# A trunk layer on one core: more weight blocks in the first stage, context tiles in a later pool, constant products first

## The chip, the core and the metric

The kernel runs on one core of a Trainium2 chip. It is one launch. The time is that of the whole execution on the device, in microseconds (us); the kernel before was run three times. PE is the matrix engine, DVE the vector engine, ACT the scalar engine, POOL the engine called GpSimd, SP the engine that issues most transfers. Each of them runs its own instructions strictly in the order in which they were put, and waits at an instruction until what it needs is there.

## The reference

One layer of a backbone over 512 latent tokens and 256 context tokens of width 1024. Cut to what matters:

```python
mx = adaln(c, w_mod, b_mod, 6)            # silu(c) @ w_mod: six rows of 1024
mc = adaln(c_ctx, w_mod, b_mod, 2)
hx = modulate(rmsnorm(x, norm1_g), mx[0], mx[1])
hc = modulate(rmsnorm(ctx, norm1_g), mc[0], mc[1])
s5p = s5_discretize(...)                  # parameters of the state-space branch
xa, xb, xcg, ux, qx, kx, vx, ga, gb, gc = split_in(hx @ w_in)
uc = hc @ w_in[:, S5 columns]
kc, vc = split(hc @ w_in[:, key and value columns])
ya = short_conv_branch(xa, xb, xcg, conv_w, conv_out)
yb = s5_output(ux, states of the scan over uc and ux, ...)
yc = neighbourhood_attention(qx, kx, vx, kc, vc, rpb) @ na_out
x = x + mx[2] * ((sigmoid(ga) * ya + sigmoid(gb) * yb + sigmoid(gc) * yc) @ w_out)
x = x + mx[5] * (relu(modulate(rmsnorm(x, norm2_g), mx[3], mx[4]) @ w1) ** 2 @ w2)
return rmsnorm(x, final_norm_g)
```

Everything is float32. A product of two float32 matrices is made of three matmuls of rounded parts: high by high, high by low, low by high.

## The kernel before, in words

**Weights.** All weights stand in the chip's memory as one stream of blocks of 1 MB, in the order of use; a block has two halves. SP fetches a block as soon as its buffer is free (`fetch`, L130 to L147). The first ten blocks belong to the first stage; they rotate through three buffers, two called raw and one rawx, so that block b waits until both halves of block b-3 are used. From block 10 on there are the two raw buffers alone. `wsplit` (L156) makes the high part wh of a half on ACT (L171) and the low part wl on DVE (L174); a unit of work then is 24 matmuls.

**First stage.** Eight steps d, one for each 128 channels. A step computes two columns of the modulation (`st_mod`, L511: 16 matmuls with 2 rows out, tile mod, which has one PSUM buffer), copies the row on ACT (L515, mrow), turns it on PE (L520) and adds constants on DVE (`st_col`, L521 to L523: colS, colA, modc). With the columns, DVE makes xr (L543), ACT its high part (L544, rg), DVE its low part (L549), and PE multiplies by the weights of the state-space input (st_m and st_a). The first xr needs the norm of x: four squares on ACT (L400), folds on DVE (L401, L405), a sum on PE (xcs), the root rcx on ACT (L411), a diagonal xdg on DVE (L372) and PE's xps (L373). The next step's `st_mod` is issued before this step's products.

**Beside it** DVE works through the parameters of the state-space branch (`gen_par`, L247 to L343, about a hundred small instructions; the sines are on ACT, L279). Its factors CFcr, CFnci, CFar and CFai feed `gen_s5e`: for each of eight blocks POOL makes products e, ta and tb (L421) and their sums (L457, L466), PE the lag products kps (L435) and the transposes etps (L442). With the last kps, DVE adds the kf rows (L479). `gen_ctx` is the norm of the context: the tile cxr (L558), squares on ACT, sums on POOL (L584 to L586, csq), PE's cps, then eight products and eight low parts on DVE (L378, L380). `gen_s5c` makes eight C blocks from transfers cb (L490), blocks 0 to 4 on DVE, 5 to 7 on POOL (tiles c and tc), and writes each to C_d.

**After it** come units in the order xa, cg, xb, uc, ga and cv and so on, with the state-space stage (stps, yps), the attention and the MLP. uc are the four context units.

The order of each engine's instructions is not written by hand: the program issues the work in the order of the code, generators being pumped between the units, and a scheduler with a model of the times then sets each engine's order. Tiles live in pools; a pool opened in the space of a closed one waits until the old tiles are no longer read. The rawx buffers, cxr and the tiles of the norms are in the start pool stp; it is closed when `gen_ctx` is through. RG are eight tiles of high and low parts of normalised channels; RG0 to RG3 hold those of the latent tokens.

Of the kernel before, what the change touches and what calls it, by code (L numbers as in the profile page):

```python
# [9 lines left out]
F32 = mybir.dt.float32  # L10
F32R = mybir.dt.float32r
I32 = mybir.dt.int32
AF = mybir.ActivationFunctionType
# [5 lines left out]
D = 1024  # L19
T = 512  # L20
TC = 256
# [54 lines left out]
def trunk(tc, xT, ctxT, cond, condT, vecs, wst, s5p, s5bc, dmat, biasA, outT):  # L76
    nc = tc.nc
# [25 lines left out]
    es = ExitStack()  # L103
    with es:
# [14 lines left out]
        def pss(name):  # L119
            return pp.tile([128, 512], F32, tag="s", bufs=1, name=name)  # L120
# [3 lines left out]
        NST = 10  # L124
        nblk = len(STREAM) // 2
# [4 lines left out]
        def fetch():  # L130
            b = st_next[0]
            back = 3 if b < NST else RAWB
            if b < nblk and (b < back or used[b - back] == 2):
                if b < NST and b % 3 == 2:
                    raws[b] = stp.tile([128, 2048], F32, tag="rawx", bufs=1, name=f"raw{b}")
                else:
                    raws[b] = wp.tile([128, 2048], F32, tag="raw", bufs=RAWB, name=f"raw{b}")
                if b < 2:
                    for o in (0, 1024):
                        nc.sync.dma_start(raws[b][:, o:o + 1024], wst[b][:, o:o + 1024])  # L140
                else:
                    nc.sync.dma_start(raws[b], wst[b])
                st_next[0] += 1
                return True
            return False
# [36 lines left out]
        RG = [gp.tile([128, 2048], F32R, name=f"rg{i}") for i in range(8)]  # L182
# [19 lines left out]
        nc.scalar.dma_start(silx, cond[0:1, :].to_broadcast([128, D]))  # L202
# [148 lines left out]
        S.activation(dum, epsc, AF.Silu)  # L351
        for _ in range(5):
            next(gpar)
# [38 lines left out]
        S.activation(silx, silx, AF.Silu)  # L392
        S.activation(dum, silx[:, 0:1], AF.Square)
# [164 lines left out]
        cxr = stp.tile([128, 8, TC], F32, tag="rawx", bufs=1, name="cxr")  # L558
        nc.sync.dma_start(cxr, ctxT)
# [19 lines left out]
        def gen_ctx():  # L579
            sq, sq2 = (stp.tile([128, 4, TC], F32, tag="sq", bufs=3, name=f"csq{i}") for i in range(2))  # L580
# [6 lines left out]
            cS = stp.tile([128, 8], F32, name="cS")  # L587
            cA = stp.tile([128, 8], F32, name="cA")
# [4 lines left out]
            rsc = rms("c", sq[:, 0], TC, stp, pss("cps"))  # L593
# [524 lines left out]
        gc = gen_ctx()  # L1118
# [11 lines left out]
        stp_cm.__exit__(None, None, None)  # L1130
# [305 lines left out]
```

## Time and profile before

| | |
|---|---|
| median of 3 runs | 1051.85 us (1051.36 to 1053.2) |
| profiled execution | 1054.51 us |
| its span, first to last instruction | 1052.7 us |
| mean granted PE clock | 0.979 |
| PE busy | 1004.4 us, 95% of the span |
| DVE, ACT, POOL busy | 558.9, 366.7, 200.7 us |
| read from memory, written | 130.16 MB, 18.32 MB |

The rows further down come from this one execution. A timeline row gives start and duration in us, engine, line, operation, what it writes and reads, how many neighbours are put together (x8), and in brackets the idle time before it and what ended that. "issue" means that the profile shows no releaser. ACTq or SPq rows are issues of transfers. A granted clock of 1.00 is 2.4 GHz, 0.50 is 1.2 GHz.

### The profile page before, as it was taken

To read this page: it belongs to the slowest core of one execution; us is meant where nothing else is said; L and a number is where in the kernel's file an instruction comes from. 1 tells how busy PE (TensorE), PEld (TensorE's weight loads), DVE (VectorE), ACT (ScalarE), POOL (GpSimd) and SP (SyncE) were. 2 spreads that over 40 slices of the span, in tenths; PEclk is the share of its full clock that TensorE was granted. 3 is DMA by queue.
4 is the path that set the end of the run, shared out by engine and by line. 5 is a ranking of instruction groups with operands and counts; after the bars stand their busy time and mean duration, and the time that the engine had idled before them with its cause. 6 is when DMAs were issued, how large, how long until landed. Compare 5 with 4: busy or idle time off the path is not lost.

```text
span 1052.7 us, 13485 instructions
## 1 busy us (share of the span) xinstructions
PE 1004.4 (95%) x5358; PEld 810.2 (77%) x5358; DVE 558.9 (53%) x927; ACT 366.7 (35%) x586; POOL 200.7 (19%) x159
## 2 busy tenths in 40 slices
PE   5889996989899999999999999999999999999997
PEld 2457885978788787777777778998888888888887
DVE  6733789348963144465467876566442234443322
ACT  5123422332222233354346444345331113333311
POOL 0555144546661013220020200000000000000000
PEclk9999999899799999999999999999999999999999
DMA  8355334785446456443254465223323223232202
GB/s 308 130 195 175 123 135 177 172 285 179 142 156 205 143 204 227 179 145 105 71 184 139 149 233 188 81 81 126 115 81 110 90 80 120 80 103 98 80 1 80
DMA packets 64543, 149.38 MB, mean 142 GB/s; under 512 B 28864, under 2 KB 41152, under 8 KB 52064
## 3 DMA queue, kind: packets, MB, share of 16 engines
q1 hardware_dynamic: 47792, 138.99, 38.4%
q10 hardware_dynamic: 16688, 9.53, 3.2%
q8 instruction: 42, 0.69, 0.3%
q14 instruction: 21, 0.17, 0.1%
HBM read 130.16 MB, written 18.32 MB: 141 GB/s over the span
## 4 chain that ended last, share of the span: by engine, by line
PE 74%; DMA 8%; DVE 8%; POOL 5%; issue 3%; ACT 2%; SPq 1%; ACTq 0%; DVEq 0%; POOLq 0%
PE m L99 10%; PE m L100 10%; PE m L101 10%; PE mod L511 3%; PE ops L829 2%; DMA raw<-in_wst_dram 2%; DMA C_d<-c 2%; PE sps L788 2%; PE ptps L814 2%; PE wo L100 1%; PE wo L99 1%; PE wo L101 1%; DVE v L681 1%; DVE wl L174 1%; DMA ks<-KT_d 1%
## 5 line engine op out<-in xcount | busy, mean ns | idle before, releaser
L174 DVE TENSOR_TENSOR wl<-raw,wh 128x1024 fp32r<-128x1024 f32 x144 | 187.6, 1303 | 226.1 <-ACT wh L171 224.4
L171 ACT CAST wh<-raw 128x1024 fp32r<-128x1024 f32 x144 | 150.9, 1049 | 314.6 <-PE m L100 151.1
L99 PE MATMUL m<-rg,wh 128*128 128x512 f32 (+1 forms) x480 | 184.2, 385 | 0.0
L101 PE MATMUL m<-rg,wl 128*128 128x512 f32 (+1 forms) x480 | 183.9, 384 | 0.0
L101 PEld LDWEIGHTS m<-rg,wl 128*128 128x128 f32 x480 | 90.1, 188 | 19.1
L99 PEld LDWEIGHTS m<-rg,wh 128*128 128x128 f32 x480 | 89.9, 188 | 18.7
L100 PE MATMUL m<-rg,wh 128*128 128x512 f32 (+1 forms) x256 | 96.4, 378 | 0.0
L100 PE MATMUL m<-actl,wh 128*128 128x512 f32 x224 | 87.8, 392 | 0.0
L1065 POOL TENSOR_TENSOR junk<-raw,silx 128x1024 f32<-128x1024 f32 x16 | 45.4, 2838 | 215.5 <-DMA raw<-in_wst_dram 214.2
L100 PEld LDWEIGHTS m<-rg,wh 128*128 128x128 f32 x256 | 48.0, 188 | 8.6
L511 PE MATMUL mod<-raw,cs 128*2 128x256 f32 x128 | 35.0, 432 | 17.9 <-DMA raw<-in_wst_dram 10.9
L100 PEld LDWEIGHTS m<-actl,wh 128*128 128x128 f32 x224 | 42.0, 187 | 9.8
L511 PEld LDWEIGHTS mod<-raw,cs 128*2 128x2 f32 x128 | 11.2, 92 | 38.1 <-issue 15.9
L1069 DVE SCALAR_TENSOR_TENSOR jk<-raw,silx 128x1024 bf16<-128x1024 f32 x16 | 21.8, 1362 | 32.5 <-DMA raw<-in_wst_dram 32.5
L1020 DVE SCALAR_TENSOR_TENSOR fg<-m,mod,fg 128x512 f32<-128x512 f32 x14 | 10.5, 751 | 52.8 <-PE m L101 52.8
L681 DVE TENSOR_TENSOR_SCAN v<-r,v 128x96 f32<-128x96 f32 x64 | 29.5, 523 | 15.1 <-POOL v L673 15.1
L92 ACT CAST rg<-relu 128x512 fp32r<-128x512 f32 (+1 forms) x36 | 20.3, 575 | 38.6 <-DVE relu L1013 38.6
L93 DVE TENSOR_TENSOR actl<-relu,rg 128x512 fp32r<-128x512 f32 (+1 forms) x36 | 22.3, 630 | 18.5 <-ACT rg L92 18.5
L100 PE MATMUL wo<-rg,wh 128*128 128x256 f32 (+1 forms) x104 | 31.8, 309 | 0.0
L99 PE MATMUL wo<-rg,wh 128*128 128x256 f32 (+1 forms) x104 | 31.8, 307 | 0.0
L101 PE MATMUL wo<-rg,wl 128*128 128x256 f32 (+1 forms) x104 | 31.5, 306 | 0.0
L829 PE MATMUL ops<-pt,v 128*64 128x128 f32 (+1 forms) x256 | 31.3, 287 | 0.0
(426 smaller groups left out, 2309.0 us busy)
## 6 DMA issues: line engine op xcount, KB each, us to landing
raw<-in_wst_dram SPq DMA_DIRECT2D x94, 1024.0 KB
E_d<-et ACTq DMA_DIRECT2D x8, 512.0 KB
C_d<-c SPq DMA_DIRECT2D x8, 512.0 KB
et<-E_d SPq DMA_DIRECT2D x8, 512.0 KB
ca<-C_d SPq DMA_DIRECT2D x8, 512.0 KB
fg<-in_xT_dram SPq DMA_DIRECT2D x4, 512.0 KB
raw<-in_wst_dram SPq DMA_DIRECT2D x4, 512.0 KB
u<-U_d SPq DMA_DIRECT2D x8, 256.0 KB
```

The costliest lines, as they stand in the source:

```text
L93: (eng or V).tensor_tensor(lo, src, f(hi), op=SUB)
L99: PE.matmul(ps, a[0], b[0], start=start, stop=False)
L100: PE.matmul(ps, a[0], b[1], start=False, stop=False)
L101: PE.matmul(ps, a[1], b[0], start=False, stop=stop)
L171: S.copy(a, src)
L174: V.tensor_tensor(b, src, f(a), op=SUB)
L511: PE.matmul(ps[0:2, 0:256], cs[:, kt], half(h)[:, 256 * (kt % 4):256 * (kt % 4) + 256], start=kt == 0, stop=kt == 7)
L681: V.tensor_tensor_scan(v[:, g, c], r8, v[:, g, c], 0.0, op0=MUL, op1=ADD)
L788: PE.matmul(ps[:, h, o:o + c1 - c0], q[r, 128 * i:128 * i + 128], k[r, c0:c1], start=True, stop=True)
L829: PE.matmul(ops[r], v[:rows, vt, r], pt[:rows, h, t], start=t == 0, stop=t == 3, skip_group_check=True)
L1065: P.tensor_tensor(junk, half(h), silx, op=MUL)
L1069: V.scalar_tensor_tensor(jk, half(h), 1.0, silx, op0=MUL, op1=MUL, accum_out=modx[:, i:i + 1])
```

## The change

`FIRST` names for each of the first ten blocks the kind of its buffer and the block that it has to wait for. The first six blocks wait for none: two have raw buffers, four rawx buffers. Blocks 6 to 9 wait for blocks 0 to 3, blocks 10 and 11 for 6 and 7. The space for the three more rawx buffers is that of RG4 to RG7, which are now made after the start pool is closed. The start pool is closed right after its last evacuations, and the tiles of `gen_ctx`, cxr among them, are in a pool of their own behind that. The transfer of silx (c, laid over all partitions for later modulation) and its Silu are issued there too. Fourteen matmuls of a constant tile with itself stand ahead of everything on PE. Nothing else is edited.

```diff
--- before.py
+++ after.py
@@ -122,6 +122,8 @@
 
         RAWB = 2
         NST = 10
+
+        FIRST = [("raw", None)] * 2 + [("rawx", None)] * 4 + [("raw", 0), ("raw", 1), ("rawx", 2), ("rawx", 3)]
         nblk = len(STREAM) // 2
         st_next = [0]
         used = [0] * nblk
@@ -129,10 +131,10 @@
 
         def fetch():
             b = st_next[0]
-            back = 3 if b < NST else RAWB
-            if b < nblk and (b < back or used[b - back] == 2):
-                if b < NST and b % 3 == 2:
-                    raws[b] = stp.tile([128, 2048], F32, tag="rawx", bufs=1, name=f"raw{b}")
+            before = FIRST[b][1] if b < NST else {10: 6, 11: 7}.get(b, b - RAWB)
+            if b < nblk and (before is None or used[before] == 2):
+                if b < NST and FIRST[b][0] == "rawx":
+                    raws[b] = stp.tile([128, 2048], F32, tag="rawx", bufs=4, name=f"raw{b}")
                 else:
                     raws[b] = wp.tile([128, 2048], F32, tag="raw", bufs=RAWB, name=f"raw{b}")
                 if b < 2:
@@ -179,7 +181,7 @@
             rest()
 
 
-        RG = [gp.tile([128, 2048], F32R, name=f"rg{i}") for i in range(8)]
+        RG = [gp.tile([128, 2048], F32R, name=f"rg{i}") for i in range(4)]
         FG = [gp.tile([128, 2048], F32, name=f"fg{i}") for i in range(2)]
 
         def gpair(h0, l0, k, n=T, per=4):
@@ -199,7 +201,6 @@
         cs = cp.tile([128, 8, 2], F32, name="cs")
         nc.scalar.dma_start(cs, condT)
         silx = tp.tile([128, D], F32, name="silx")
-        nc.scalar.dma_start(silx, cond[0:1, :].to_broadcast([128, D]))
         for c in range(4):
             nc.sync.dma_start(FG[c // 2].rearrange("p (a t) -> p a t", a=4)[:, 2 * (c % 2):2 * (c % 2) + 2], xT[:, 2 * c:2 * c + 2])
             if c == 1:
@@ -349,6 +350,9 @@
         par_cm = tc.tile_pool(name="s5par", bufs=1)
         gpar = gen_par(par_cm.__enter__(), keepp)
         S.activation(dum, epsc, AF.Silu)
+        wps = pss("warm")
+        for i in range(14):
+            PE.matmul(wps[:, 0:128], ones, ones, start=True, stop=True)
         for _ in range(5):
             next(gpar)
 
@@ -389,8 +393,7 @@
 
 
         S.activation(cs, cs, AF.Silu)
-        S.activation(silx, silx, AF.Silu)
-        S.activation(dum, silx[:, 0:1], AF.Square)
+        S.activation(dum, cs[:, 0, 0:1], AF.Square)
 
         xs = [FG[c // 2][:, (c % 2) * 1024:(c % 2) * 1024 + 1024] for c in range(4)]
         xcs = pm("xcs")
@@ -555,8 +558,6 @@
             st_pump(3 if ST_GENS[0] is gpar else 1)
             if d == 7:
                 wsplit(UNITS[0])
-        cxr = stp.tile([128, 8, TC], F32, tag="rawx", bufs=1, name="cxr")
-        nc.sync.dma_start(cxr, ctxT)
 
 
         U_d = tc.dram_tile([4, 8, 128, 128], F32, name="U_d")
@@ -576,21 +577,24 @@
                 ev_u(j)
 
 
-        def gen_ctx():
-            sq, sq2 = (stp.tile([128, 4, TC], F32, tag="sq", bufs=3, name=f"csq{i}") for i in range(2))
+        def gen_ctx(stc):
+            cxr = stc.tile([128, 8, TC], F32, name="cxr")
+            nc.sync.dma_start(cxr, ctxT)
+            S.activation(silx, silx, AF.Silu)
+            sq, sq2 = (stc.tile([128, 4, TC], F32, tag="sq", bufs=2, name=f"csq{i}") for i in range(2))
             S.activation(sq, cxr[:, 0:4], AF.Square)
             S.activation(sq2, cxr[:, 4:8], AF.Square)
             yield
             P.tensor_tensor(sq, sq, sq2, op=ADD)
             P.tensor_tensor(sq[:, 0:2], sq[:, 0:2], sq[:, 2:4], op=ADD)
             P.tensor_tensor(sq[:, 0], sq[:, 0], sq[:, 1], op=ADD)
-            cS = stp.tile([128, 8], F32, name="cS")
-            cA = stp.tile([128, 8], F32, name="cA")
+            cS = stc.tile([128, 8], F32, name="cS")
+            cA = stc.tile([128, 8], F32, name="cA")
             V.tensor_tensor(cS, modc[:, 0:8], vec[:, 0:8], op=ADD)
             V.tensor_tensor(cA, modc[:, 8:16], b1, op=ADD)
             V.tensor_tensor(cA, cA, g1, op=MUL)
             yield
-            rsc = rms("c", sq[:, 0], TC, stp, pss("cps"))
+            rsc = rms("c", sq[:, 0], TC, stc, pss("cps"))
             yield
             for d in range(0, 8, 2):
                 for e in (d, d + 1):
@@ -1115,7 +1119,12 @@
 
         where = {u: i for i, u in enumerate(UNITS)}
         start_evac()
-        gc = gen_ctx()
+        stp_cm.__exit__(None, None, None)
+        gp2 = es.enter_context(tc.tile_pool(name="gran2", bufs=1, side="right"))
+        RG += [gp2.tile([128, 2048], F32R, name=f"rg{i}") for i in range(4, 8)]
+        stc_cm = tc.tile_pool(name="startc", bufs=1, side="right")
+        gc = gen_ctx(stc_cm.__enter__())
+        nc.scalar.dma_start(silx, cond[0:1, :].to_broadcast([128, D]))
         gens.append(gc)
         gm = gen_mod()
         gens.append(gm)
@@ -1127,7 +1136,7 @@
             assert UNITS[i][0] != "uc"
             slot(i)
             i += 1
-        stp_cm.__exit__(None, None, None)
+        stc_cm.__exit__(None, None, None)
         s5c_cm = tc.tile_pool(name="s5c", bufs=1, side="right")
         gcc = gen_s5c(s5c_cm.__enter__())
         gens.append(gcc)
```

Lines of the changed kernel are a few higher than those before. At three places the order of the instructions shows the change.

On ACT, in the first stage before (sq are the squares, mrow the copied modulation row, wh a cast, rcx the root of the norm, prm a sine):

```order
L400 ACTIVATE sq_164<-fg_81 128x1024
L392 ACTIVATE silx<-silx 128x1024
L393 ACTIVATE dum<-silx 128x1
L410 ACT_TABLE_LOAD
L410 ACTIVATE dum<-dum 128x1
L400 ACTIVATE sq_172<-fg_82 128x1024
L400 ACTIVATE sq_175<-fg_82 128x1024
L515 COPY mrow_211<-mod_200 2x256
L171 CAST wh_237<-raw_96 128x1024
L411 ACTIVATE rcx<-rcx,epsc 128x4
L279 ACT_TABLE_LOAD
L279 ACTIVATE prm<-prm 128x32
```

and now:

```order
L413 ACT_TABLE_LOAD
L413 ACTIVATE dum<-dum 128x1
L403 ACTIVATE sq_187<-fg_78 128x1024
L518 COPY mrow_226<-mod_215 2x256
L583 ACT_TABLE_LOAD
L583 ACTIVATE silx<-silx 128x1024
L403 ACTIVATE sq_190<-fg_78 128x1024
L173 CAST wh_252<-raw_91 128x1024
L280 ACTIVATE prm<-prm 128x32
L281 ACTIVATE prm<-prm 128x32
L414 ACT_TABLE_LOAD
L414 ACTIVATE rcx<-rcx,epsc 128x4
```

The load of silx's Silu and that Silu now stand between the third square and the fourth, and a load stands directly ahead of the root, behind the sines.

On PE, in the first stage before, from the end of the products of step 1 (st_m, st_a) to those of step 2; mod_340 is the modulation of step 3, kps the lag products of block 0:

```order
L100 MATMUL st_a<-rg_75,wh_237 128x512
L101 MATMUL st_a<-rg_73,wl_238 128x512
L520 MATMUL mod_277<-ident,mrow_288 128x2 x2
L511 MATMUL mod_340<-raw_241,cs 2x256 x8
L99 MATMUL st_m_218<-rg_73,wh_354 128x512
L99 MATMUL st_m_219<-rg_73,wh_354 128x512
L99 MATMUL st_m_220<-rg_73,wh_354 128x512
```

and now, where mod_355 is the modulation of step 3:

```order
L100 MATMUL st_a<-rg_75,wh_252 128x512
L101 MATMUL st_a<-rg_73,wl_253 128x512
L438 MATMUL kps_612<-bc_506,e_510 128x32
L514 MATMUL mod_355<-raw_98,cs 2x256 x8
L438 MATMUL kps_612<-bc_506,e_510 128x32 x5
L99 MATMUL st_m_233<-rg_73,wh_369 128x512
L99 MATMUL st_m_234<-rg_73,wh_369 128x512
```

Before, the kps rows began one step later, behind the products of step 2. The first kps matmul, which reads POOL's e, has moved ahead of the modulation of step 3.

On POOL, near the end of the context units before (e_1285 is the last e, tc and c the first C block made on POOL):

```order
L457 TENSOR_TENSOR e_1285<-e_1285,ta_1286 128x512
L421 TENSOR_TENSOR tc_1436<-cb_1404,CFai 128x512
L421 TENSOR_TENSOR tb_1339<-bc_1174,CFcr 128x512
L466 TENSOR_TENSOR e_1285<-e_1285,tb_1339 128x512
L421 TENSOR_TENSOR c_1406<-cb_1404,CFar 128x512
L421 TENSOR_TENSOR c_1406<-cb_1404,CFai 128x512
```

and now:

```order
L460 TENSOR_TENSOR e_1307<-e_1307,ta_1308 128x512
L424 TENSOR_TENSOR tb_1361<-bc_1196,CFcr 128x512
L469 TENSOR_TENSOR e_1307<-e_1307,tb_1361 128x512
L424 TENSOR_TENSOR tc_1458<-cb_1426,CFai 128x512
L424 TENSOR_TENSOR c_1428<-cb_1426,CFar 128x512
L424 TENSOR_TENSOR c_1428<-cb_1426,CFai 128x512
```

tb and the last sum of e have moved ahead of the first C product.

## Rows read from the trace of the kernel before

**Rows 1.** Busy time by stretch (stretch, its length, engines, PE clock, DMA share, GB/s).

```profile
core 0: us, PE busy (x) PEld busy (x) DVE busy (x) ACT busy (x) POOL busy (x), PEclk, DMA share, GB/s
20.00:40.00 20.00, 16.85 (x66) 8.01 (x65) 19.31 (x76) 5.41 (x10) 2.31 (x2) 0.91 0.52 194
100.00:170.00 70.00, 69.45 (x341) 57.56 (x340) 55.80 (x71) 24.82 (x35) 27.54 (x19) 1.00 0.37 127
170.00:200.00 30.00, 20.72 (x136) 19.65 (x135) 19.75 (x21) 9.45 (x14) 18.29 (x14) 0.83 0.58 193
200.00:230.00 30.00, 29.12 (x129) 23.79 (x128) 10.99 (x12) 11.71 (x15) 10.29 (x10) 1.00 0.89 230
230.00:291.00 61.00, 54.96 (x393) 46.57 (x392) 52.01 (x90) 18.24 (x34) 38.82 (x41) 0.86 0.54 176
330.00:1052.00 722.00, 712.53 (x3740) 583.41 (x3738) 343.68 (x523) 262.46 (x427) 46.39 (x18) 1.00 0.36 124
```

**Rows 2.** Timeline of PE, modulation matmuls (start, duration, engine, line, idle before, releaser).

```profile
10.94 3.57 PE L511 MATMUL mod<-raw,cs 128*2 128x256 f32 x8 [10.94 <-DMA raw<-in_wst_dram]
...
41.54 5.30 PE L511 MATMUL mod<-raw,cs 128*2 128x256 f32 x16 [4.00 <-issue]
...
50.63 3.61 PE L511 MATMUL mod<-raw,cs 128*2 128x256 f32 x16 [0.28 <-issue]
...
78.86 5.30 PE L511 MATMUL mod<-raw,cs 128*2 128x256 f32 x16 [2.44 <-issue]
```

**Rows 3.** Timeline of DVE, first xr, column step 2, a weight split.

```profile
24.92 0.75 DVE L543 SCALAR_TENSOR_TENSOR xr<-fg,colA,xps 128x512 f32<-128x512 f32 x1 [0.19 <-PE xps L373]
...
41.03 0.16 DVE L521 TENSOR_TENSOR colS<-mod,vec 128x1 f32<-128x1 f32 x1
...
76.50 1.93 DVE L174 TENSOR_TENSOR wl<-raw,wh 128x1024 fp32r<-128x1024 f32 x1 [5.82 <-ACT wh L171]
```

**Rows 4.** Timeline of ACT in the first stage.

```profile
10.31 1.28 ACT L410 ACT_TABLE_LOAD   x1
...
11.60 0.20 ACT L410 ACTIVATE dum<-dum 128x1 f32<-128x1 f32 x1
...
15.94 1.06 ACT L400 ACTIVATE sq<-fg 128x1024 f32<-128x1024 f32 x1 [0.52 <-DMA fg<-in_xT_dram]
...
17.38 0.36 ACT L515 COPY mrow<-mod 2x256 f32<-2x256 f32 x1 [0.39 <-PE mod L511]
...
20.71 0.30 ACT L411 ACTIVATE rcx<-rcx,epsc 128x4 f32<-128x4 f32 x1 [2.02 <-DVE rcx L409]
...
75.43 1.99 ACT L171 CAST wh<-raw 128x1024 fp32r<-128x1024 f32 x2 [2.68 <-DMA raw<-in_wst_dram]
```

**Rows 5.** Timeline of POOL, first e product and sum, first context sum.

```profile
40.79 1.05 POOL L421 TENSOR_TENSOR ta<-bc,CFnci 128x512 f32<-128x512 f32 x1 [1.07 <-DVE CFnci L340]
...
44.81 2.24 POOL L457 TENSOR_TENSOR e<-e,ta 128x512 f32<-128x512 f32 x1
...
102.83 2.39 POOL L584 TENSOR_TENSOR csq<-csq,csq 128x1024 f32<-128x1024 f32 x1
```

**Rows 6.** Timeline of PE, the last kps block and the first ga matmul.

```profile
184.63 0.63 PE L435 MATMUL kps<-bc,e 128*128 128x32 f32 x2 [5.07 <-POOL e L466]
...
199.19 0.40 PE L99 MATMUL ga<-rg,wh 128*128 128x512 f32 x1
```

**Rows 7.** Timeline of POOL, its first C product and its last e.

```profile
179.00 1.91 POOL L421 TENSOR_TENSOR tc<-cb,CFai 128x512 f32<-128x512 f32 x1 [9.17 <-ACT rg L92]
...
182.45 2.13 POOL L466 TENSOR_TENSOR e<-e,tb 128x512 f32<-128x512 f32 x1
```

**Rows 8.** Timeline of ACT, first cb transfer's issue, cast for the last context unit.

```profile
120.77 1.27 ACTq L490 DMA_DIRECT2D cb<-in_s5bc_dram  x2
...
189.83 1.05 ACT L171 CAST wh<-raw 128x1024 fp32r<-128x1024 f32 x1 [6.21 <-POOL tc L421]
```

**Rows 9.** Timeline of DVE, last sum of C block 4, first kf row.

```profile
178.18 0.68 DVE L498 TENSOR_TENSOR c<-c,tc 128x512 f32<-128x512 f32 x1
...
199.03 1.10 DVE L479 TENSOR_TENSOR kf<-kf,dmt 16x512 f32<-16x512 f32 x1 [1.74 <-DMA KT_d<-kev]
```

## The prediction

> **What bounds the kernel now.** I read the page's first two parts, then busy time by stretch, then the early timelines of PE, DVE, ACT and POOL, and last the same engines around the largest hole. From 330 us on PE runs 712.53 of 722 us at full clock [rows 1], so nothing can be won there, and what is gained or lost before should arrive at the end unchanged. What PE loses lies in the first stage, from 170 to 200 us (20.72 of 30 us busy, clock 0.83) and from 230 to 291 us (54.96 of 61, clock 0.86) [rows 1].
>
> In the first stage the reader is to see who is waited for. The modulation matmuls of step 3 start 4.00 us late and then run at half clock (16 in 5.30 us, against 3.61 us in step 4), and the same happens before step 7: 2.44 us late, again 5.30 us [rows 2]. The profile calls both "issue". The tile that these matmuls write has one buffer, and what frees it is the column step on DVE, L521 to L523. For step 3 that runs at 41.03 us [rows 3], behind the S5 parameter chain, with next to no gap: DVE is busy 19.31 of 20 us from 20 to 40 us [rows 1]. For step 7 it stands behind a weight split that waited for its cast on ACT [rows 3], and that cast waited for a transfer of a raw block [rows 4]. So of the two stalls the block supply made only the second.
>
> **Part by part.** The sum is made against the profiled execution (1054.51 us, of which 1052.7 us are span); the median 1051.85 us is 2.7 us lower.
>
> *Six blocks.* They can save the second stall and its half clock: 2.44 + (5.30 - 3.61) = 4.1 us. The first stall is DVE's and stays. The silx transfer (0.5 MB) now goes out behind the first square, which lets block 0 land perhaps 0.5 us before 10.94 us [rows 2]; I put the row copy of step 0 at 17.0 instead of 17.38 us [rows 4].
>
> *Silx on ACT.* In the new order the Silu of silx, with a table load of its own, stands ahead of the fourth square, and the load that the root rcx needs directly ahead of rcx; before, all Silu work came first. From 17.4 us: load 1.28, Silu (as large as a square) 1.06, square 1.06 [rows 4] put the end of that square at 20.8 us; it was 15.94 + 1.06 = 17.0 us, 3.8 us earlier. With the load before rcx it is 5.1 us: rcx ends near 26.1 instead of 21.0 us [rows 4]. The first xr, which needs rcx through a diagonal and PE, is ready at 24.92 + 5.1 = 30.0 us [rows 3]. DVE covers part of this: some 25 more parameter rows and a weight split now stand ahead of the first xr. The parameters lose only what DVE cannot fill. I take a gap of 2.2 us (about 1.2 of it because the sines come later), less the 0.7 us of a low part that now stands behind them: the last factor that POOL waits for is late by 1.5 us. This matters because PE's order now has the first kps matmul ahead of the modulation of step 3. It needs POOL's sum, which ended at 44.81 + 2.24 = 47.05 us [rows 5]; 1.5 us later that is 48.6 us. Step 3 then starts at 48.6 instead of 41.54 us: +7.1 us. The bounds are 0 (kps finds its operand ready, and the column step comes as before) and 9 us (the whole detour of 5.1 us plus the split of 1.9 us now ahead of that column step plus 2 us of gap). With the 4.1 us off, the first stage ends 3 us later, bounds -4 and +9. One block of kps and etps more moves from later into this stage; what it adds here is missing there.
>
> The Trainium skill has a rule on the loads ("ScalarE: Activation LUTs", What ACT_TABLE_LOAD costs): a switch costs about 1.28 us plus a drain of some 1.38 us. The row of the load agrees with the first figure, but the next instruction starts 0.01 us after the load's end [rows 4], so no such drain shows here; by the page's sum two loads would cost 2.8 us more, and the forecast would be at most that much higher.
>
> *Constant products.* Nothing that the rest waits for reads the fourteen 128-column matmuls. Step 0 ran at half clock, its first eight matmuls in 3.57 us where sixteen later took 3.61 [rows 2]. At best the products save 3.57 - 3.61 / 2 = 1.8 us; at worst nothing, since PE idles again from their end (near 7 us) until block 0 is there. I take 0, because the idle times before steps 3 and 7 were both followed by half clock [rows 2].
>
> The skill's page "TensorE: Matmul & The Clock Gate" (Part 1) says that the throttled clock is the default and that activity releases it; by that alone the products would buy the 1.8 us, and the forecast would be 1044 us.
>
> *Context tiles.* Their pool can only open when the start pool closes, and that waits for the four U_d writes. The POOL sums, which began at 102.83 us [rows 5] on data long landed, I move back by the writes, the transfer and two squares, some 12 us, and with them everything up to the first C block (its transfer at 120.77 us [rows 8], then near 135). PE's order has the context norm after the xa units, so PE itself waits 0 to 2.5 us; I take 0.5.
>
> *170 to 200 us.* Here lies the gain. PE's longest wait, 5.07 us, is for POOL's last e [rows 6]. That e stood behind tc, the first C product on POOL, before which POOL sat idle 9.17 us until 179.00 us; e ended at 182.45 + 2.13 = 184.58 us [rows 7]. In the new order e and its tb stand ahead of tc, so POOL makes them in its idle time and PE's wait goes. Next late is the weight chain. The cast for the last context unit waited until 189.83 us, queued on ACT behind a cb transfer, which waited for POOL [rows 8]. The two POOL instructions that leave that path took 184.58 - (179.00 + 1.91) = 3.7 us [rows 7]. So the cast comes at 186.1 us, the low part near 187.2, that of the next unit 2 to 4 us later, and ga starts near 191.5 instead of 199.19 us [rows 6], if DVE is through with its xb splits by 186 us as before. DVE idled 14.2 of the 70 us from 100 to 170 [rows 1]; the later context norm uses up most of that, but the xb splits also come about one C block earlier in DVE's queue. Next late is a row on DVE fed by a transfer, kf (199.03 us [rows 9]), which now stands ahead of the low parts for ga: +1.5 us, if the transfer takes 1 to 2 us as its wait of 1.74 us suggests. So ga starts at 193 us, 6.2 us earlier. The 3.5 us from the first stage and the context are in that: they arrive in PE's hole of 9.3 us and its half clock, and are absorbed. Bounds: 0 (tc comes later by as much as e gave back) and -10 (PE never waits after 171 us and keeps its clock).
>
> *After 200 us.* From 230 to 291 us PE idles 6.0 us and at clock 0.86 loses some 8 more; DVE is busy for 52.01 of these 61 us [rows 1]. An earlier ga may keep or shift these waits. I count 0, with bounds -4 (a third of the loss goes) and +5 (it grows by as much as the first part's).
>
> Sum: 1054.5 - 6.2 = 1048.3 us profiled; about 1046 us in the median.
>
> **Rivals.** (a) The block supply binds throughout stage one. Then both stalls and both half clocks go, 4.00 + 2.44 + 2 x 1.69 = 9.8 us, and with C blocks that start sooner part of the hole at 170 us too, some 3 us: 1039 us. For it: the wait before step 7. Against: DVE without gaps from 20 to 40 us. Chance 0.10.
>
> (b) The gain is given back: the stretch from 230 to 291 us is paced by DVE, and an earlier ga only lengthens PE's waits there. Time 1052 us. For it: 52.01 of 61 us. Against: DVE idles 19 of the 30 us before [rows 1], so its work can start earlier as well. Chance 0.16.
>
> (c) Slower: the C blocks. If the five on DVE keep the 58 us that they took from the first transfer at 120.77 us [rows 8] to the last sum at 178.9 us [rows 9], but begin 13 us later because of the context pool, tc starts at 192 us. The cast for the last context unit follows after 189.83 - 179.00 - 3.7 = 7.1 us, at 199.1, and ga 9.4 us behind it as before, at 208.5 instead of 199.2: +9.3 us, 1061 us, or 1056 at half of it. It decides as soon as the fifth C block ends later than 178.9 + 3.7 = 182.6 us. For it: one in-order queue carries C blocks, splits and evacuations. Against: the idle time of DVE before 170 us. Chance 0.22.
>
> **How the numbers follow.** The likeliest case, 0.52, gives 1046 us, by itself 1039 to 1050. (a) has 0.10, (b) 0.16, (c) 0.22. A measurement of this kernel can tell 0.2% or 2.1 us from no change: below 1049.7 is faster, above 1054 slower. The likeliest case and (a) give faster 0.62; most of (b) is within, 0.14; its rest and (c) are slower, 0.24. The range 1037 to 1058 leaves out the far part of (a) and what of (c) exceeds two thirds of its price, about a tenth each.
>
> **What would show it.** Right: the fourth square ends near 20.8 us and the first xr starts near 33; the modulation of step 3 starts at 47 to 50 us, behind a kps that waits for POOL; no stall before step 7; the first C product near 138 us; POOL's last e done before 180 us with no PE wait for it; ga at 190 to 196 us. Wrong: step 3 at or before 41.5 us (then (a)), the fifth C block after 186 us (then (c)), or ga early with a hole of 10 us and more between 225 and 300 us (then (b)).

## The result, and the profile after

| | before | changed |
|---|---|---|
| median of ten runs each | 1052.19 us (1051.15 to 1055.59) | 1046.28 us (1042.52 to 1049.55) |
| ratio to before, 95% interval | | 0.9935 [0.9915, 0.9954] |
| profiled execution, its span | 1054.51, 1052.7 us | 1049.55, 1047.8 us |
| first xa matmul | 95.4 us | 100.7 us |
| first xb | 142.3 | 144.7 |
| first uc | 171.8 | 172.2 |
| first ga | 199.2 | 187.5 |
| first gc | 361.9 | 355.4 |

The change is 0.65% faster, near the 1046 us that were forecast. The lower part of the table is what it is made of, read from PE's timelines of the two profiled executions (first starts of each tile): the first stage ends later, 0.4 us is left of that at uc, the changed kernel is 11.7 us ahead at the start of ga, and 5.2 us of these are given back before gc. From gc to the end it takes another 1.6 us more (692.4 against 690.8 us), so the two spans differ by 4.9 us, and the medians by 5.9.

A single run, 1232.37 us of the swap with lag writes on POOL (further down), ran at a mean granted clock of 0.754; it is in that row's median and not in its ratio.

Busy time by stretch of the changed kernel, to be held against [rows 1]:

```profile
core 0: us, PE busy (x) PEld busy (x) DVE busy (x) ACT busy (x) POOL busy (x), PEclk, DMA share, GB/s
20.00:40.00 20.00, 15.64 (x54) 7.38 (x55) 18.42 (x69) 6.21 (x11) 2.72 (x2) 0.78 0.70 280
100.00:170.00 70.00, 70.00 (x335) 58.24 (x335) 53.12 (x74) 25.38 (x36) 25.72 (x18) 1.00 0.42 137
170.00:200.00 30.00, 28.38 (x187) 25.02 (x186) 22.06 (x25) 10.67 (x16) 9.92 (x8) 1.00 0.86 225
200.00:230.00 30.00, 27.87 (x116) 22.50 (x115) 12.94 (x10) 9.57 (x11) 16.64 (x13) 0.94 0.70 227
230.00:291.00 61.00, 51.66 (x381) 43.80 (x380) 48.06 (x87) 18.64 (x32) 38.26 (x41) 0.92 0.51 171
330.00:1047.00 717.00, 706.68 (x3723) 578.53 (x3721) 342.17 (x521) 259.89 (x424) 45.67 (x18) 1.00 0.36 123
```

The hole from 170 to 200 us is closed: 28.38 of 30 us busy at full clock, against 20.72 at 0.83. From 200 to 291 us PE idles 2.13 + 9.34 us instead of 0.88 + 6.04. From 20 to 40 us, PE now idles and runs slower than before (15.64 us busy, clock 0.78, against 16.85 and 0.91).

The first stage on PE, against [rows 2]: the constant products, step 0, step 2 behind its column step, the kps that waits for POOL, steps 3, 6 and 7.

```profile
1.05 5.20 PE L355 MATMUL warm<-ones 128*128 128x128 f32 x28 [1.05 <-DVE hpi L220]
...
8.31 3.54 PE L514 MATMUL mod<-raw,cs 128*2 128x256 f32 x8 [2.06 <-DMA raw<-in_wst_dram]
...
32.75 5.00 PE L514 MATMUL mod<-raw,cs 128*2 128x256 f32 x16 [4.34 <-DVE modc L526]
...
46.72 0.41 PE L438 MATMUL kps<-bc,e 128*128 128x32 f32 x2 [2.03 <-POOL e L460]
...
47.06 3.62 PE L514 MATMUL mod<-raw,cs 128*2 128x256 f32 x16
...
75.80 5.30 PE L514 MATMUL mod<-raw,cs 128*2 128x256 f32 x16
...
85.79 3.61 PE L514 MATMUL mod<-raw,cs 128*2 128x256 f32 x16 [0.62 <-PE mod L523]
```

Step 3 starts at 47.06 us, directly behind the kps that waited 2.03 us for POOL's sum; before, it was 41.54. Step 7 has lost its stall; half clock is now in step 6. The constant products (14 issued, which the trace counts as 28) end at 6.25 us, 2.06 us before block 0 lands, and in this execution step 0 runs at half clock all the same (its first 8 matmuls in 3.54 us, granted clock 0.53; before 3.57 us, where the profile reads 1.00 and only the duration tells). The repetition of this kernel, further down, shows another step 0.

ACT in the first stage, against [rows 4], and then DVE, against [rows 3]:

```profile
14.69 0.36 ACT L518 COPY mrow<-mod 2x256 f32<-2x256 f32 x1 [1.97 <-PE mod L514]
...
15.07 1.28 ACT L583 ACT_TABLE_LOAD   x1
...
17.32 1.04 ACT L403 ACTIVATE sq<-fg 128x1024 f32<-128x1024 f32 x1
...
23.55 0.30 ACT L414 ACTIVATE rcx<-rcx,epsc 128x4 f32<-128x4 f32 x1
```

```profile
31.53 0.75 DVE L546 SCALAR_TENSOR_TENSOR xr<-fg,colA,xps 128x512 f32<-128x512 f32 x1
```

The row copy of step 0 comes at 14.69 instead of 17.38 us, since block 0 lands 2.6 us sooner. Behind it stand the load and the Silu of silx, then the fourth square; rcx ends at 23.85 us (21.01 before), the first xr starts at 31.53 (24.92 before).

From 100 to 200 us, first POOL, against [rows 5] and [rows 7], then ACT, against [rows 8], and DVE's low part for the last context unit:

```profile
114.78 2.41 POOL L588 TENSOR_TENSOR csq<-csq,csq 128x1024 f32<-128x1024 f32 x1 [8.75 <-ACT csq L586]
...
170.69 1.63 POOL L469 TENSOR_TENSOR e<-e,tb 128x512 f32<-128x512 f32 x1
...
185.55 1.38 POOL L424 TENSOR_TENSOR tc<-cb,CFai 128x512 f32<-128x512 f32 x1 [13.23 <-DVE c L501]
```

```profile
134.73 0.84 ACTq L493 DMA_DIRECT2D cb<-in_s5bc_dram  x2
...
179.21 1.05 ACT L173 CAST wh<-raw 128x1024 fp32r<-128x1024 f32 x1
...
184.72 0.35 ACTq L493 DMA_DIRECT2D cb<-in_s5bc_dram  x1
```

```profile
182.87 1.22 DVE L176 TENSOR_TENSOR wl<-raw,wh 128x1024 fp32r<-128x1024 f32 x1
```

The context sums begin 12.0 us later, the cb transfers at 134.73 instead of 120.77 us, the first C product on POOL at 185.55 instead of 179.00 us, and for it POOL sat idle 13.23 us. But e is done at 172.32 us, so PE does not wait for it, and the cast for the last context unit (179.21 us; 189.83 before) stands ahead of the cb transfer that waits for POOL (184.72 us).

### The profile page after: what moved, and what is told of

The parts are those of the page before. It is cut to its first block, busy times and chain, and to the rows that moved or that the text cites. A ratio compares the mean times of both kernels' runs of the same rounds, so it can differ in the third digit from the quotient of the medians.

```text
span 1047.8 us, 13544 instructions
## 1 busy us (share of the span) xinstructions
PE 1005.8 (96%) x5386; PEld 811.9 (77%) x5386; DVE 557.8 (53%) x927; ACT 366.8 (35%) x586; POOL 202.1 (19%) x159
## 4 chain that ended last, share of the span: by engine, by line
PE 78%; DMA 8%; DVE 6%; POOL 3%; ACT 2%; issue 1%; SPq 1%; ACTq 0%; DVEq 0%; POOLq 0%
PE m L99 10%; PE m L100 10%; PE m L101 10%; DMA raw<-in_wst_dram 3%; PE mod L514 2%; PE ops L833 2%; PE sps L792 1%; PE wo L99 1%; PE wo L100 1%; PE wo L101 1%; PE gb L99 1%; PE gb L100 1%; PE gb L101 1%; DMA ks<-KT_d 1%; DVE v L685 1%
## 5 line engine op out<-in xcount | busy, mean ns | idle before, releaser
L176 DVE TENSOR_TENSOR wl<-raw,wh 128x1024 fp32r<-128x1024 f32 x144 | 191.3, 1329 | 221.9 <-ACT wh L173 213.6
```

The source lines that it names most:

```text
L176: V.tensor_tensor(b, src, f(a), op=SUB)
```

## The experiments

Each run was timed beside the kernel before on its own chip; the ratio with its interval is to that. Single runs of the kernel before spread from 1046.9 to 1061.8 us here, so medians and intervals decide, and traces, which are of one execution, are read for where things stand, not for the last 2 or 3 us.

| run | median us | before | ratio, 95% interval |
|---|---|---|---|
| swap alone | 1052.49 | 1052.81 | 0.9993 [0.9965, 1.0021] |
| changed, silx early | 1049.59 | 1052.81 | 0.9972 [0.9950, 0.9994] |
| the same without constant products | 1049.25 | 1052.81 | 0.9966 [0.9940, 0.9992] |
| changed, three buffers | 1051.27 | 1052.81 | 0.9987 [0.9965, 1.0009] |
| changed, again | 1047.06 | 1053.13 | 0.9929 [0.9904, 0.9954] |
| context pool alone | 1048.15 | 1053.13 | 0.9949 [0.9926, 0.9973] |
| changed, supply of three | 1045.96 | 1053.13 | 0.9915 [0.9887, 0.9944] |
| changed, u on ACT | 1046.99 | 1053.13 | 0.9932 [0.9906, 0.9957] |
| swap, lag writes on POOL | 1059.95 | 1052.84 | 1.0074 [1.0046, 1.0102] |
| changed, lag writes on POOL | 1052.55 | 1052.84 | 1.0007 [0.9981, 1.0033] |
| changed, u, ca, ks on ACT | 1048.74 | 1052.84 | 0.9969 [0.9948, 0.9990] |
| both of these | 1051.60 | 1052.84 | 0.9995 [0.9975, 1.0016] |

**Swap alone.** To the kernel before; the order of every engine but POOL stays, and on POOL one instruction moves.

```diff
-                    P.tensor_tensor(e1[:, 1], e1[:, 1], ta, op=SUB)
+                    order[f"e{b}"] = P.tensor_tensor(e1[:, 1], e1[:, 1], ta, op=SUB)
...
-                    prod(eng, ta, C[:, 1], y, b)
+                    with after("e7" if b == 5 and c == 0 else None):
+                        prod(eng, ta, C[:, 1], y, b)
```

> The kernel before with one swap: POOL's first C product stands behind tb and the last sum of e; every other instruction keeps its place. Theory (the gain is this swap): PE's 5.07 us wait for e goes, ga starts at 191 to 195 instead of 199.2 us, and of that 3 to 6 us arrive at the end: 1046 to 1049 us. Rival (the gain comes from weights that lie ready early, the swap is a bystander): the next wait, for a cast or a low part, takes the place of the one removed; ga within 1.5 us of 199.2, 1051 to 1053 us.

PE's wait for e is gone and ga starts at 192.9 us, 6.3 us earlier, in the middle of what the theory gave. But gc starts at 360.4 us, and the median does not move. So my theory, that the swap is the gain, fell: the place was right, the price was not. A part of where it went shows on SP, ACT and PE of this run:

```profile
190.17 0.33 SPq L142 DMA_DIRECT2D raw<-in_wst_dram  x1
...
191.28 13.15 SPq L483 DMA_DIRECT2D KT_d<-kev  x13
...
204.55 0.87 SPq L142 DMA_DIRECT2D raw<-in_wst_dram  x1
```

```profile
213.15 1.04 ACT L171 CAST wh<-raw 128x1024 fp32r<-128x1024 f32 x1 [4.79 <-DMA raw<-in_wst_dram]
```

```profile
214.75 0.50 PE L99 MATMUL ga<-rg,wh 128*128 128x512 f32 x1 [2.46 <-ACT tga L955]
```

SP puts thirteen writes of lag products (KT_d) between two raw blocks; the second goes out at 204.55 us, only 2 us earlier than before (206.50 us in that trace), and the cast for ga's next unit waits 4.79 us for it (3.80 us before). In the changed kernel that raw block is issued at 199.19 us. Whether the lag writes are the cause is tested further down.

**Silx early, with and without constant products.** To the changed kernel:

```diff
+        nc.scalar.dma_start(silx, cond[0:1, :].to_broadcast([128, D]))
...
-        S.activation(dum, cs[:, 0, 0:1], AF.Square)
+        S.activation(silx, silx, AF.Silu)
+        S.activation(dum, silx[:, 0:1], AF.Square)
...
-            S.activation(silx, silx, AF.Silu)
...
-        nc.scalar.dma_start(silx, cond[0:1, :].to_broadcast([128, D]))
```

and in the second run also

```diff
-        wps = pss("warm")
-        for i in range(14):
-            PE.matmul(wps[:, 0:128], ones, ones, start=True, stop=True)
```

> The changed kernel with silx's transfer and Silu back at their old place, all else changed. Theory (the detour on ACT costs the first stage its time): the fourth square ends by 17 us, the first xr starts 3 to 5 us earlier than at 31.5 us, step 3 at 42 to 44 instead of 47.06 us, the context units some 3 us earlier, the end 1 to 4 us earlier: 1042 to 1045 us. Rival (the first stage has room to absorb it): first stage ends within 1 us of the changed kernel's, the time stays at 1045 to 1048 us.

> As the run with silx at its old place, and without the fourteen constant products. Theory (they end too early to matter): step 0 starts at the same time and its first eight matmuls take 3.5 to 3.6 us with and without them, the time is within 1.5 us of the run with silx at its old place. Rival (they hold the clock up): without them step 0 is 1.8 us longer than with them, and the end is 1 to 2 us later.

Without the detour, step 3 starts at 44.58 us and not at 47.06, but block 0 lands at 10.22 instead of 8.31 us, so the first stage's part of the expectation came true by half. Of these 2.5 us 0.2 are left at the first xa (100.5 us) and at the first uc (172.0 us): that much the rival had right. The end is not earlier, though; by the medians it is later than the changed kernel's (0.9972 against 0.9935, and against 0.9929 on another chip, with intervals that overlap a little). In the trace of this run a new wait stands in the context units, PE's etps for ACT's copy et, 2.67 us, and ga starts at 191.5 us. So no price of the detour is seen at the end, and moving it changed the order 130 us further on.

No gain from the constant products is seen at the end, 1049.59 us with and 1049.25 without, but each interval is some 2 us to either side and could hide the 1.8 us that was their best case. In the two traces, on the same chip, step 0:

```profile
10.22 2.47 PE L516 MATMUL mod<-raw,cs 128*2 128x256 f32 x8 [4.12 <-DMA raw<-in_wst_dram]
...
14.42 3.57 PE L516 MATMUL mod<-raw,cs 128*2 128x256 f32 x8
```

```profile
10.06 3.25 PE L513 MATMUL mod<-raw,cs 128*2 128x256 f32 x8 [10.06 <-DMA raw<-in_wst_dram]
...
14.22 1.89 PE L513 MATMUL mod<-raw,cs 128*2 128x256 f32 x8
```

With them the first eight matmuls take 2.47 instead of 3.25 us, and the second eight 3.57 instead of 1.89: the clock was up for a while (granted 0.74 from 10.2 to 12.7 us) and had fallen when the second half ran (0.50 from 14.4 to 18.0 us). The 3.5 to 3.6 us that I expected with and without them is in neither trace. What the products leave also differs between executions of one kernel. In the repetition of the changed kernel they end later and step 0 runs at full clock:

```profile
1.05 6.29 PE L355 MATMUL warm<-ones 128*128 128x128 f32 x28 [1.05 <-DVE hpi L220]
8.32 1.89 PE L514 MATMUL mod<-raw,cs 128*2 128x256 f32 x8 [0.98 <-DMA raw<-in_wst_dram]
```

Of the nine traces with the products, five have 1.89 us there, three 3.44 to 3.57, and this one 2.47; the five without them have 3.25 to 3.57. The Trainium skill says in "TensorE: Matmul & The Clock Gate" (Part 1) that activity releases the throttled clock. The five traces at 1.89 us agree; the other four show that it does not always last until block 0 is there.

**Three buffers.** To the changed kernel:

```diff
-        FIRST = [("raw", None)] * 2 + [("rawx", None)] * 4 + [("raw", 0), ("raw", 1), ("rawx", 2), ("rawx", 3)]
+        FIRST = [(("raw", "raw", "rawx")[b % 3], b - 3 if b > 2 else None) for b in range(10)]
...
-            before = FIRST[b][1] if b < NST else {10: 6, 11: 7}.get(b, b - RAWB)
+            before = FIRST[b][1] if b < NST else {10: 7, 11: 9}.get(b, b - RAWB)
...
-                    raws[b] = stp.tile([128, 2048], F32, tag="rawx", bufs=4, name=f"raw{b}")
+                    raws[b] = stp.tile([128, 2048], F32, tag="rawx", bufs=1, name=f"raw{b}")
```

> The changed kernel with the first ten blocks back on three buffers (block b waits for block b-3), all else changed, so context tiles in the later pool, silx late, constant products first. Theory (six blocks save only the stall before step 7 with its half clock, 4.1 us, in the first stage, part of which is absorbed later): first stage up to 4 us longer, the end 0 to 4 us later than the changed kernel's: 1046 to 1050 us. Rival (the blocks carry the gain): the end at 1051 us or later.

The gain is gone within the interval, and that looked like the rival. But the trace shows another difference. With 24 KB per partition less in the start pool, the context tiles no longer wait for it:

```profile
23.99 3.00 POOL L588 TENSOR_TENSOR csq<-csq,csq 128x1024 f32<-128x1024 f32 x1 [22.69 <-ACT csq L586]
...
164.44 1.06 POOL L424 TENSOR_TENSOR tc<-cb,CFai 128x512 f32<-128x512 f32 x1 [49.15 <-DVE c L501]
```

```profile
179.28 0.41 PE L438 MATMUL kps<-bc,e 128*128 128x32 f32 x2 [2.51 <-POOL e L460]
...
186.19 3.19 PE L438 MATMUL kps<-bc,e 128*128 128x32 f32 x14 [5.46 <-POOL e L469]
```

The context sums run at 23.99 us and not at 114.78, C blocks are early, POOL's order has the first C product ahead of e again, and PE waits 2.51 + 5.46 us for POOL. Memory and supply were changed together, so this run could not tell them apart. The next two can.

**The changed kernel again, the context pool alone, a supply of three.** The second is the kernel before with

```diff
-        cxr = stp.tile([128, 8, TC], F32, tag="rawx", bufs=1, name="cxr")
-        nc.sync.dma_start(cxr, ctxT)
...
-        def gen_ctx():
-            sq, sq2 = (stp.tile([128, 4, TC], F32, tag="sq", bufs=3, name=f"csq{i}") for i in range(2))
+        def gen_ctx(stc):
+            cxr = stc.tile([128, 8, TC], F32, name="cxr")
+            nc.sync.dma_start(cxr, ctxT)
+            sq, sq2 = (stc.tile([128, 4, TC], F32, tag="sq", bufs=2, name=f"csq{i}") for i in range(2))
...
-        gc = gen_ctx()
+        stp_cm.__exit__(None, None, None)
+        stc_cm = tc.tile_pool(name="startc", bufs=1, side="right")
+        gc = gen_ctx(stc_cm.__enter__())
```

the third the changed kernel with the three buffers' `FIRST` and `before` as above and

```diff
+        RX = []
...
-                    raws[b] = stp.tile([128, 2048], F32, tag="rawx", bufs=4, name=f"raw{b}")
+                    if not RX:
+                        RX.extend(stp.tile([128, 2048], F32, name=f"rawx{i}") for i in range(4))
+                    raws[b] = RX[0]
```

> The changed kernel once more, on the chip of the next three runs, so that they can be compared with it. All theories: 0.5 to 0.8% faster than before, as measured; ga from 186 to 190 us, the first gc unit near 355 us.

> The kernel before with one part of the change: the context tiles in a pool behind the start pool. Three buffers, silx early, no constant products. The order that results has POOL's e ahead of tc, and DVE's C blocks about one block later against the xb and uc work. Theory 2 (the hole from 170 to 200 us closes when both the swap and the later C blocks are there, and that is what the change brings): ga at 188 to 193 us, 3 to 6 us less at the end, 1046 to 1049 us against 1052. Rival (the six blocks as a supply carry the gain): hole smaller, but time within 2 us of before, as with the swap alone.

> The changed kernel in the same memory layout and nearly the same order, but the four rawx buffers used as one, so that block b waits for block b-3 as before. Theory 2 (supply is not what gains): the casts of blocks 2 and 3 and the step before 7 wait some 2 to 4 us more, first stage 1 to 4 us longer, the time 0 to 2 us above the changed kernel's. Rival (supply carries the gain): 5 us and more above it, so 1051 us or later.

The changed kernel repeats its result. With the memory held and only the supply back at three blocks, the time is the same, 0.9915 against 0.9929: the six blocks as a supply show no gain at the end. The stall before step 7 is back, as foreseen, and so are the closed hole and the early ga:

```profile
83.36 5.29 PE L517 MATMUL mod<-raw,cs 128*2 128x256 f32 x16 [2.43 <-issue]
...
186.77 0.46 PE L99 MATMUL ga<-rg,wh 128*128 128x512 f32 x1
```

```profile
core 0: us, PE busy (x) PEld busy (x) DVE busy (x) ACT busy (x) POOL busy (x), PEclk, DMA share, GB/s
170.00:200.00 30.00, 28.57 (x185) 25.19 (x184) 21.12 (x25) 10.65 (x17) 10.27 (x7) 1.00 0.87 228
```

The context pool alone makes the kernel before 0.5% faster, most of the change's gain, with three buffers, silx early and no constant products. Its order has POOL's e ahead of tc, context sums at 113.05 us, and tc at 186.06 us, much as in the changed kernel. But its hole is only partly closed (24.89 of 30 us busy from 170 to 200 us, clock 0.83), ga starts at 196.5 us, not at the 188 to 193 that I expected, and gc at 362.7 us, no earlier than before (361.9). Its traced execution was one of 1053.52 us, 5 us above the median of that run, so its trace cannot show where the 5 us come from; the interval of its ratio and that of the swap alone overlap a little.

**Loads and writes on other queues.** To the changed kernel, u (`nc.sync` to `nc.scalar`), then u, ca and ks; then the KT_d writes from `nc.sync` to `nc.gpsimd`, in the swap alone, in the changed kernel, and with the loads:

```diff
-                nc.sync.dma_start(u, U_d[q // 2].rearrange("s (n h g) m -> (s n) h g m", n=16, h=2)[:, q % 2])
+                nc.scalar.dma_start(u, U_d[q // 2].rearrange("s (n h g) m -> (s n) h g m", n=16, h=2)[:, q % 2])
...
-                nc.sync.dma_start(KT_d[:, :, i:i + 16].rearrange("g n m -> n g m"), kev[16 * s:16 * s + 16, e])
+                nc.gpsimd.dma_start(KT_d[:, :, i:i + 16].rearrange("g n m -> n g m"), kev[16 * s:16 * s + 16, e])
```

> The changed kernel with one edit: the transfers of u in the state-space stage are issued by ACT instead of SP, where one of them stood behind a raw block's issue that waits for a low part on DVE. Theory (this queueing takes back what was gained at ga): PE's wait of 6.46 us for u near 284 us goes, and the half clock behind it (some 5 us), so 4 to 10 us less than the changed kernel: 1037 to 1042 us. Rival (DVE paces the stage from 240 to 300 us): the wait moves to another matmul there, time within 2 us of the changed kernel.

> The kernel with the swap alone, and the fifteen lag writes to KT_d issued by POOL instead of SP. Theory 3 (with the swap alone the gain at ga was lost because the next raw block's issue on SP stood behind thirteen of these writes, at 204.55 us, 2 us earlier than before, so that a cast waited 4.79 us for it): that raw block is issued at 195 to 202 us, the cast no longer waits at 213 us, the first gc unit starts at 355 to 358 instead of 360.4 us, 1047 to 1050 us. Rival (the transfer engines are full there, or the writes hold up POOL's C blocks): the block lands no sooner or the state-space stage starts later, and the time stays within 2 us of the swap alone, 1050 us and more.

> The changed kernel, with the lag writes issued by POOL instead of SP. Theory 3: the raw block of 199 us and the one after it go out earlier, the waits of ga after 200 us (2.1 and 1.5 us) go, 1 to 3 us less than the changed kernel, 1043 to 1046 us. Rival: the writes push POOL's C blocks and with them the state-space stage, 1047 us or more.

> The changed kernel with the transfers of u, ca and ks of the state-space stage on ACT, so that none of the three stands behind a raw block's issue on SP. With u alone on ACT the wait near 284 us moved to ks. Theory (the raw block's issue is what holds them): both waits go, and with them the half clock, 4 to 9 us less than the changed kernel, 1038 to 1043 us. Rival (DVE paces this stretch, whatever the queue): another wait of about the same size stands there, time within 2 us of the changed kernel.

> The changed kernel with both edits: lag writes on POOL, and u, ca and ks on ACT. If both theories hold, the two gains add: 1035 to 1041 us. If neither holds, 1045 to 1049 us.

None of them gained. The changed kernel's largest wait behind 200 us is on a u that SP issues behind a raw block:

```profile
278.47 0.33 SPq L144 DMA_DIRECT2D raw<-in_wst_dram  x1
...
278.90 0.38 SPq L631 DMA_DIRECT2D u<-U_d  x1
```

```profile
284.58 0.39 PE L660 MATMUL stps<-u,et 128*64 128x96 f32 x1 [6.46 <-DMA u<-U_d]
```

In the kernel before, the same matmul waits

```profile
278.32 0.39 PE L656 MATMUL stps<-u,et 128*64 128x96 f32 x1 [3.47 <-DMA u<-U_d]
```

With u on ACT it is issued at 275.95 us, 3 us earlier, because there it stands with ACT's tables, which wait for POOL; PE's wait moves to ks, and with ks on ACT too, two waits of 3.35 and 2.29 us stand in place of one:

```profile
275.86 0.53 ACT L649 ACTIVATE tb<-rr 128x384 f32<-128x384 f32 x1 [8.02 <-POOL rr L648]
...
275.95 0.33 ACTq L631 DMA_DIRECT2D u<-U_d  x1
```

```profile
283.71 0.66 PE L707 MATMUL yps<-u,ks 128*128 128x64 f32 x2 [4.67 <-DMA ks<-KT_d]
```

```profile
282.61 0.66 PE L707 MATMUL yps<-u,ks 128*128 128x64 f32 x2 [3.35 <-DMA ks<-KT_d]
...
286.93 0.69 PE L707 MATMUL yps<-u,ks 128*128 128x64 f32 x2 [2.29 <-DMA ks<-KT_d]
```

So the rival's time came true, and the queue alone does not pace the stretch. The rows point to the chain of DVE, POOL and ACT (ACT's table waits 8.02 us for POOL's rr); no run here shortened that chain, so this half of the rival is not shown.

The lag writes on POOL did what the theory asked of SP: the raw block goes out at 201.69 instead of 204.55 us in the swap, at 194.25 instead of 199.19 us in the changed kernel, and no cast waits for it. But they cost POOL itself: in the changed kernel eleven of them take 7.01 us there at 180.69 us, the C blocks come behind (POOL's second at 217.68 instead of 209.19 us). They cost ACT as well, which issues the context units' writes to U_d in the same stretch: the last three pairs of these take 15.21 us of ACT's queue instead of 5.94, the casts for ga stand behind them, and PE waits for ACT's tga, which comes behind such a cast:

```profile
198.09 5.76 ACTq L955 DMA_DIRECT2D U_d<-uc_sb  x2
...
203.95 1.04 ACT L173 CAST wh<-raw 128x1024 fp32r<-128x1024 f32 x1 [5.89 <-issue]
```

```profile
206.95 0.53 PE L99 MATMUL cv<-rg,wh 128*128 128x512 f32 x1 [4.68 <-ACT tga L958]
```

The gain is gone, though the hole before ga is as closed as in the changed kernel (ga at 185.9 us); the kernel with the swap became 0.7% slower than before. So these two runs cannot tell what the writes on SP cost, since moving them made new waits elsewhere. The Trainium skill says in "DMA: Bandwidth & Descriptors" (Issuing engines are not separate DMA queues) that issuing from several engines saves only the sequencer's time, usually small beside the transfer. The run agrees: u went out 3 us earlier from ACT, and the median stayed (1046.99 against 1047.06 us).

## Why the prediction was right

The time was right, by two misses that cancel, so the closeness of 1046 to 1046.28 us is luck.

- *Six blocks save the stall before step 7, the first stall stays.* Shown: 0.62 us of wait before step 7 and full clock there, against 2.43 us and half clock with a supply of three; step 2 and kps now carry the first stall (4.34 and 2.03 us). That nothing of it is seen at the end is shown by that same run.
- *The detour on ACT.* The mechanism is shown by the rows: the fourth square behind silx's Silu, xr behind 25 parameter rows, kps ahead of step 3 and waiting for POOL's sum (predicted for 48.6 us, 46.67 measured). One term was mis-sized: block 0 lands 2.6 us sooner than before, where I took 0.5 (1.9 us sooner than with silx early in the changed kernel, the one difference there). So the fourth square ends at 18.36 us instead of the 20.8 predicted, rcx at 23.85 instead of 26.1, the first xr starts at 31.53 instead of 33, and the last factor that POOL waits for is 0.3 us early, not 1.5 late (ta at 40.46, before 40.79). The first stage's lag, +3 us predicted and one block of lag work apart, was +5.3 us at the first xa, with that block in it, and +2.4 us at the first xb.
- *Constant products.* I took 0, and none of their 1.8 us is seen at the end. The reason that I gave, half clock behind the idle time, holds in only four of the nine traces with them, in one of these in part; in the other five step 0's first half takes 1.89 us.
- *Absorbed at uc.* +0.4 us there; right. The run with silx early confirms it: 2.5 us at step 3, 0.2 at uc.
- *Context tiles.* 12 us predicted, 12.0 measured; cb near 135, 134.73. No wait of PE.
- *170 to 200 us.* The sign and the place were right, the size was not: ga at 187.5 us, where I had 193 and a bound of 189. The step that failed is the sentence on the weight chain, which kept the cast for the last context unit behind a cb transfer. In the new order it stands ahead of that (179.21 against 184.72 us), so neither 3.7 us less nor kf's 1.5 us more mattered. The low part came at 182.87 us, and PE had no wait for it.
- *After 200 us.* I counted 0 and gave +5 as the bound; 11.7 us at ga became 6.5 at gc, so 5.2 us went. This is the second miss. A part of it is the longer wait for u, 6.46 us where it was 3.47 before. The last C block of that stage was written 4.4 us later (issue at 228.94 against 224.50 us); that this is the reason is not shown. The rest is spread over small waits for low parts and ACT from the start of ga on (0.47, 1.00 and 2.13 us, against 0.88 before).

Of the rivals, (a) is ruled out by the supply of three. (b) was nearly whole in the swap alone (6.3 us at ga, 1.5 left at gc) and half in the changed kernel. (c) met its own condition: the fifth C block ended at 185.4 us, later than 182.6. Its consequence did not follow, for the reason just given: the cast no longer stood behind POOL.

What I had named as the gain, e ahead of tc, takes PE's wait for e away in the traces (where tc is first, it stands there: 5.07 us before, 5.46 with three buffers) but is not enough: alone it changed the time by -0.07%, with an interval from -0.35 to +0.21%. By the medians the context pool carries most of the gain. That it does so by putting the context norm, and with it DVE's C blocks, behind the work of xb and uc is read from the order and not shown: the closed hole itself, ga at 185.9 to 187.9 us, is in the traces of the changed kernel and of the runs that keep its memory, silx and constant products, and in one of these, with the lag writes on POOL, nothing of the time is won. It stays open why the context pool alone, whose hole in its trace is about as large as that of the swap alone, ended some 4 us earlier in the median.

## What to carry to other kernels

Where a scheduler sets the order, an edit's largest effect can lie far from it: here a change of pools, meant to make room for weights, moved a norm by 12 us, and most of the gain came with it, while the six blocks as a supply gave none that is seen. Undo parts one at a time with the memory held as it is, or two causes look like one. And a wait that is removed on the bound engine is worth only what the next supply behind it allows: follow the weights' issue, cast and low part past the hole before a gain is booked.

## What was not expected of the hardware

A 0.5 MB transfer on ACT's queue (silx), issued 4 us later, let step 0 start sooner on the first weight block: at 8.12 to 8.65 us in the eight traces with silx late, at 10.06 to 10.94 us in the six with it early. In the pair that differs in nothing else it is 8.31 against 10.22 us.

In the changed kernel's first stage half clock followed idle times of 2.06, 4.58 and 4.34 us, but also, in step 6 (5.30 us for 16 matmuls), a wait of only 0.97 us, while step 3 behind a wait of 2.03 us ran at full clock. In the repetition of the same kernel, behind waits of 2.05 and 0.95 us, it is the other way round, so the wait alone does not tell which step is slow:

```profile
45.65 6.50 PE L514 MATMUL mod<-raw,cs 128*2 128x256 f32 x16
...
77.25 3.62 PE L514 MATMUL mod<-raw,cs 128*2 128x256 f32 x16
```

Small-row writes (KT_d) issued by POOL took about 0.64 us each of POOL's own time (eleven in 7.01 us), against about 1.0 us each on SP (thirteen in 13.15 us). With all fifteen on POOL, the last six of ACT's writes to U_d took 15.21 us of its queue instead of 5.94 in the changed kernel, whose ratio went from 0.9929 to 1.0007, and the kernel with the swap went from 0.9993 to 1.0074.
